# Hybrid attention step: row maxima of mixer A from 64 rows instead of 128, two heads side by side in the two row halves of the array

## The chip, the core and the metric

One core of a Trainium2 chip. The metric is the device time of one execution in microseconds. The engines are named as in the profile: PE multiplies matrices, DVE is the vector engine, ACT the scalar engine, POOL the GpSimd engine, SP issues most DMAs; PEld is PE's weight load, which runs beside its matmuls.

## What is computed

One layer of a diffusion backbone on 128 context tokens (tile 0) and 1024 latent tokens (tiles 1 to 8). After a modulated RMS norm and one input projection there are two attention branches with 8 query heads on 2 key groups each, head size 64. Mixer A is global: each latent query sees all 1024 latent keys and 128 cached context keys. Mixer B sees a window of 128 to either side and the context, with a sink logit. The gated results go through one output projection.

```python
def one_block(qblk):                      # mixer A, per 128 latent queries
    s = jnp.einsum('bqkgd,bskd->bkgqs', qblk, k_all).astype(jnp.float32) * (d ** -0.5)
    p = jax.nn.softmax(s, axis=-1).astype(v_all.dtype)
    return jnp.einsum('bkgqs,bskd->bqkgd', p, v_all)
```

Subtracting any per-row constant before the exponential leaves a softmax unchanged. The kernel subtracts a row maximum of the scores, and that row maximum is what the change touches.

## The kernel before

**Number format.** Every fp32 operand is split into a high part and a low part (`hi`, `lo`), and the products that matter are summed. Queries lie in DRAM as `q_dram[t][m]`, 128 rows: rows 0 to 63 the high parts of the 64 head dimensions, rows 64 to 127 the low parts; the columns are heads, 128 queries each. `u_load` (line 832) brings the four heads of one unit into a tile `qt` of 128 x 512. The keys `kha` hold the high part twice, in rows 0 to 63 and again in 64 to 127, so that a 128-row product gives (q_hi + q_lo) · k_hi.

**Units and slots.** Attention runs over 36 units `(t, m, g)`: token tile, mixer, key group. For each latent tile come unit (A, g0), (B, g0), (A, g1), (B, g1); so an A unit and a B unit alternate, and unit `i` of mixer A has an even number. The four prompt units come last. A unit is a row of slots, one per key block: 9 for mixer A, mostly 4 for mixer B. Below, A0 to A8 are the slots of an A unit and B0 to B3 those of the B unit behind it. The recording loop does in each slot, in this order: what was put off to this slot (`later`), the slot's score matmuls (`scores`), the due items (`due`), some matmuls of the output projection (`po`, 2.5 per slot while there are any), and the value matmuls of the slot three earlier (`values`, LAG = 3). In an A slot the scores are two matmuls (lines 1097 and 1098); `ACT` then takes the exponential (1100) and the high part (1104), and POOL or DVE the low part. In a B slot they are four transposes (1092) of probabilities that were computed earlier. The order in which instructions are recorded is kept on every engine (`in_order`).

**What precedes an A unit.** Its row maxima must be known before its slot A0. For latent tiles, `max_items` makes 12 items out of them, one for each head `h` and each third `b` of the 9 key blocks: a matmul of 128 rows into 384 columns (line 858) and a DVE maximum (859). The table `MX_AT` says in which slots they stand, counted from the start of the A unit two units earlier: five of them in the B unit before that (-4, -3, -2, -2, -1), seven in A4, A5, A5, A7, A7, A8, A8. Then `finish` loads the tile `qb` and takes the negative maximum `m_nat`; two ticks later `transpose` turns it on PE (877, `ptm`) and DVE writes it into four rows of `qb` (878). Units 0 and 2 have their items beside the last gate projection (`EARLY`).

**What precedes a B unit.** `weight_items` puts one head in each of A0 to A3: two matmuls into `sn` (915, 916), a DVE operation with mask and maximum (919), and, from the next slot on, an ACT exponential with its row sum (905, written `pen`, followed by a read of the accumulator). In B1 `pti` (967) turns the inverse sums on PE, and ACT copies them out (971).

**Banks.** The PSUM tag "A" has two banks, taken in turn. In this part of the kernel `pmx`, `sn`, `pti` and `ptm` all take their bank from it: a matmul that writes a bank waits until the last reader of what stood there is done.

Of the kernel before, what the change touches and what calls it, by code (L numbers as in the profile page):

```python
# [9 lines left out]
F32 = mybir.dt.float32  # L10
# [3 lines left out]
ALU = mybir.AluOpType  # L14
AX = mybir.AxisListType
# [3 lines left out]
P = 128  # L19
# [22 lines left out]

NAT_AT = (0, 1, 2, 3)
NAT_FIRST = (0, 1, 2, 3)
MX_AT = (-4, -3, -2, -2, -1, 4, 5, 5, 7, 7, 8, 8)
MX_FIRST = (0, 1, 2, 2, 3, 4, 4, 5, 6, 6, 7, 8)
PH_DVE = 0
MX_END = 10
SPLIT_LAG = 2
# [58 lines left out]
def hybrid_step(ctx, tc, x_prompt, x_sample, cache_k_a, cache_v_a, cache_k_b, cache_v_b,  # L108
# [3 lines left out]
    nc = tc.nc  # L112
# [5 lines left out]
    q_dram = [[dram.tile([P, 1024], F32, name=f"qd{t}_{m}") for m in range(2)] for t in range(NT)]  # L118
# [7 lines left out]
    def later(n, f):  # L126

        agenda.setdefault(now[0] + n, []).append(f)
# [13 lines left out]
    def bank(tag, name):  # L142
        return ps.tile([P, 512], F32, tag=tag, name=name, bufs=BANKS[tag])
# [167 lines left out]
    with tc.tile_pool(name="st", bufs=2, side="right") as st:  # L311
# [129 lines left out]
        for j in range(KT + 2):  # L441
# [42 lines left out]
            if X_FROM + 1 < j <= X_FROM + 4:  # L484
                t = rest[j - X_FROM - 2]
# [8 lines left out]
            if KT - 2 <= j < KT:  # L494
# [3 lines left out]
                c0, n = W_QA.cols[0]  # L498
# [52 lines left out]
    with tc.tile_pool(name="qt", bufs=2, side="right") as qt:  # L551
# [90 lines left out]
        for m in range(2):  # L642
            w, nxt = ((W_QA, W_QB), (W_QB, W_KV))[m]
            ts = list(range(1, NT)) + [0]
            for t in ts:
# [3 lines left out]
                if (m, t) in ((0, ts[-2]), (1, ts[GATE_AT[0]])):  # L649
                    n = len(wg) // 2  # L650
# [28 lines left out]
    kha = kv.tile([P, 2, 9, P], F32R, name="kha")  # L679
# [3 lines left out]
    khp = kv.tile([P, 4, P], F32R, name="khp")  # L683
# [139 lines left out]
    qs = ctx.enter_context(tc.tile_pool(name="qs", bufs=2, side="right"))  # L823
# [5 lines left out]
    qtile, qbtile, mxtile, sgl = {}, {}, {}, {}  # L829
# [4 lines left out]
    def u_load(i):  # L834
        t, m, g = units[i]
        more = i % QTS > 3
        qt_ = (qp2[0] if more else qp).tile([P, 512], F32R, tag="qt", name=f"qt{i}", bufs=QTS - 4 if more else 4)
        nc.sync.dma_start(qt_.bitcast(F32), q_dram[t][m][:, 512 * g : 512 * g + 512])
        qtile[i] = qt_

    def max_items(i):

        t, m, g = units[i]
        out = []

        def item(h, b):
            if h == 0 and b == 0:
                mxtile[i] = qs.tile([P, 4, 3], F32, tag="mx", name=f"mx{i}", bufs=3)
            mx = mxtile[i]
            lhs = qtile[i][:, P * h : P * h + P]  # L850
            pm = bank("A", f"pmx{i}_{h}_{b}")
            if t == 0:
                for h in range(4):
                    hs = slice(P * h, P * h + P)
                    nc.tensor.matmul(pm[:, hs], qtile[i][:, hs], khp[:, g, :], start=True, stop=True)
                nc.vector.tensor_reduce(mx[:, :, 0], pm.rearrange("p (h n) -> p h n", h=4), axis=AX.X, op=ALU.max)
            else:
                nc.tensor.matmul(pm[:, 0:384], lhs, kha[:, g, 3 * b : 3 * b + 3, :], start=True, stop=True)  # L858
                nc.vector.tensor_reduce(mx[:, h, b : b + 1], pm[:, 0:384], axis=AX.X, op=ALU.max)  # L859

        def finish():
            qb_ = qp.tile([68, 512], F32R, tag="qb", name=f"qb{i}", bufs=2)
            nc.sync.dma_start(qb_[0:64, :].bitcast(F32), q_dram[t][m][0:64, 512 * g : 512 * g + 512])
            qbtile[i] = qb_
            mx = mxtile.pop(i)
            mn = m_nat[i // 2 % 2]
            if t > 0:
                m4 = qs.tile([P, 4], F32, tag="m4", name=f"m4{i}", bufs=3)
                nc.vector.tensor_reduce(m4, mx, axis=AX.X, op=ALU.max)
            else:  # L870
                m4 = mx[:, :, 0]
            nc.vector.tensor_scalar(mn, m4, -1.0, None, op0=ALU.mult)
            later(TURN, transpose)

        def transpose():
            pt = bank("A", f"ptm{i}")
            nc.tensor.transpose(pt[0:4, 0:P].bitcast(F32R), m_nat[i // 2 % 2], ident_r)
            nc.vector.tensor_tensor(qbtile[i][64:68, :].rearrange("p (h n) -> p h n", h=4),  # L878
                                    pt[0:4, 0:P].unsqueeze(1).to_broadcast([4, 4, P]),
                                    diag.unsqueeze(2).to_broadcast([4, 4, P]), op=ALU.mult)  # L880

        for h in range(4 if t else 1):
            for b in range(3 if t > 0 else 1):
                out.append(lambda h=h, b=b: item(h, b))
        return out, finish

    def weight_items(i):

# [133 lines left out]
    for i in range(LOADED):  # L1022
        u_load(i)
    for i in EARLY:
        items, end = max_items(i)
        beside[2] += items + [end]
# [14 lines left out]
    for f in beside[2]:  # L1041
# [5 lines left out]
        name=nc.get_next_instruction_name(), engine=mybir.EngineType.Activation, act_func_set_id=6))  # L1047
# [155 lines left out]
    slots, start = [], []  # L1203
# [8 lines left out]
    def put(s, f):  # L1212
        due.setdefault(s, []).append(f)

    for i, (t, m, g) in enumerate(units):
        if i in EARLY:
            continue
        if m == 0:
            items, done = max_items(i)
            at, end = [start[i - 2] + a for a in (MX_AT if i > 2 else MX_FIRST)], start[i - 2] + MX_END  # L1220
            if t == 0:
                end = start[i] - LEAD
                at = [end - 1]
        else:
            items, done = weight_items(i)
            at = [start[i - 1] + j for j in (NAT_AT if i > 1 else NAT_FIRST)] if t else [start[i] - PROMPT_LEAD]
            end = at[-1] + 1
        if i >= LOADED:
            first = max(start[i - QTS + 1] - 1, at[0] - LOADLEAD, 0)
            assert first < at[0] or first == 0, (i, first, at)  # L1230
            put(first, lambda i=i: u_load(i))
        for s, f in zip(at, items):
            put(s, f)
        put(end, done)
# [88 lines left out]
```

## Time and profile before

| | |
|---|---|
| median of 3 runs | 723.58 us (723.54 to 723.71) |
| span of the profiled execution | 721.3 us |
| busy | PE 698.3 us (97%), DVE 457.6 (63%), ACT 411.7 (57%), POOL 335.3 (46%) |
| weight loads (PEld) | 559.7 us (78%) |
| DMA | 78.56 MB, mean 109 GB/s |

The profiled execution has no time of its own beside its span of 721.3 us; the median of the three runs is 2.3 us more than that span, which is what lies around it. Busy times are unions of the instructions' durations on one engine. A matmul's modelled end lies beyond the start of the next one, so the pace of PE is read from the starts: the time from one start to the next.

### The profile page before, as it was taken

Reading aid. Unit: us, or ns where it says so; the run is one execution under the profiler, and the core shown is the slowest. Engines: PE = TensorE matmul, PEld = TensorE weight load, DVE = VectorE, ACT = ScalarE, POOL = GpSimd, SP = SyncE. Lnnn points to the kernel's source line nnn. Section 1 sums busy time; section 2 is a strip of 40 time slices with the busy share of each in tenths; the row PEclk is TensorE's granted clock in tenths of the full one; section 3 lists DMA queues with packets and bytes.
Section 4 is the critical chain, followed back from the end, with each engine's and each line's share of the span. In section 5 each row is a group of like instructions: output and inputs, shape, how many; then the busy total and the mean of one; then the engine's idle time right before and its main releaser. Section 6 shows DMA issues by size and latency. Waiting matters only on the chain. (4 is left out here: it accounts for less than half of the span.)

```text
span 721.3 us, 10622 instructions
## 1 busy us (share of the span) xinstructions
PE 698.3 (97%) x3524; PEld 559.7 (78%) x3524; DVE 457.6 (63%) x1007; ACT 411.7 (57%) x829; POOL 335.3 (46%) x355
## 2 busy tenths in 40 slices
PE   5999999999999999999999999999999999999997
PEld 2678988877777788977788888888888888887865
DVE  3466147875675872745866677577666775775653
ACT  5355411411232451158778877877787778877770
POOL 3456013332322340236666555655575557555751
PEclk9999999999999999999999999999999999999999
DMA  8961373348435115440321222121212221212323
GB/s 344 346 219 59 121 278 86 79 94 276 121 85 142 45 60 171 139 143 23 103 67 45 73 67 88 44 81 52 87 54 59 66 87 45 81 53 87 103 65 119
DMA packets 53159, 78.56 MB, mean 109 GB/s; under 512 B 6569, under 2 KB 25449, under 8 KB 52081
## 3 DMA queue, kind: packets, MB, share of 16 engines
q1 hardware_dynamic: 44928, 65.96, 28.1%
q10 hardware_dynamic: 8176, 11.94, 6.3%
q8 instruction: 28, 0.46, 0.3%
q14 instruction: 27, 0.21, 0.1%
HBM read 58.69 MB, written 19.18 MB: 108 GB/s over the span
## 5 line engine op out<-in xcount | busy, mean ns | idle before, releaser
L1108 POOL TENSOR_TENSOR pl<-pe,ph 128x512 fp32r<-128x512 f32 x130 | 167.6, 1292 | 144.7 <-DVE nm L919 67.5
L859 DVE TENSOR_REDUCE mx<-pmx 128x1 f32<-128x384 f32 x192 | 101.4, 552 | 59.5 <-PE pmx L858 58.1
L1100 ACT ACTIVATE pe<-st 128x512 f32<-128x512 f32 x146 | 86.8, 594 | 28.0 <-PE st L1098 27.1
L1104 ACT CAST ph<-pe 128x512 fp32r<-128x512 f32 x146 | 90.6, 621 | 4.8
L1118 PE MATMUL pv<-ph,v_hi 128*128 128x512 f32 x208 | 83.2, 400 | 2.2 <-DVE spare L1142 2.2
L1121 PE MATMUL pv<-pl,v_hi 128*128 128x512 f32 x208 | 82.6, 397 | 0.0
L173 POOL TENSOR_TENSOR rs_q<-ms_q,mhalf 128x8 f32<-128x8 f32 x18 | 34.8, 1931 | 82.1 <-DVE ms_q L171 82.1
L1189 PE MATMUL po<-wo,ogh 128*128 128x512 f32 x216 | 72.5, 394 | 0.2 <-DVE yt L1196 0.2
L919 DVE CUSTOM_DVE_ANT_0 sn<-sn,mask,nsink 128x512 f32<-128x512 f32 (+1 forms) x64 | 46.3, 724 | 38.3 <-PE sn L916 36.5
L858 PE MATMUL pmx<-kha,qt 128*128 128x384 f32 x192 | 61.0, 363 | 0.4 <-ACT pen L905 0.2
L1097 PE MATMUL st<-qt,kha 128*128 128x512 f32 x144 | 58.3, 405 | 1.5 <-ACT pe L1100 0.8
L1098 PE MATMUL st<-qb,kla 68*128 68x512 f32 x144 | 57.6, 400 | 1.1 <-DVE qb L878 1.1
L1120 PE MATMUL pv<-ph,v_lo 128*64 128x512 f32 x146 | 57.9, 396 | 0.0
L1121 PEld LDWEIGHTS pv<-pl,v_hi 128*128 128x128 f32 x208 | 39.4, 189 | 16.7 <-issue 0.2
L905 ACT ACTIVATE pen<-sn,nm 128x512 f32<-128x512 f32 (+2 forms) x72 | 45.0, 626 | 6.5 <-DVE nm L919 3.1
L1093 ACT CAST ph<-st 128x512 fp32r<-128x512 f32 x62 | 36.4, 587 | 19.9 <-PE st L1092 18.7
L1118 PEld LDWEIGHTS pv<-ph,v_hi 128*128 128x128 f32 x208 | 39.4, 189 | 10.5 <-ACT ogh L1154 2.4
L1189 PEld LDWEIGHTS po<-wo,ogh 128*128 128x128 f32 x216 | 40.0, 188 | 6.8 <-DVE yt L1196 0.6
L1094 DVE TENSOR_TENSOR pl<-st,ph 128x512 fp32r<-128x512 f32 x62 | 42.5, 686 | 2.3 <-ACT ph L1093 1.5
L1189 PE MATMUL po<-wo,ogl 128*128 128x512 f32 x108 | 42.6, 394 | 0.0
L594 ACT ACTIVATE sqq<-pq 128x512 f32<-128x512 f32 x18 | 10.8, 599 | 53.3 <-DMA qd<-qo0q 14.4
L858 PEld LDWEIGHTS pmx<-kha,qt 128*128 128x128 f32 x192 | 35.5, 190 | 6.2 <-DVE mx L859 1.4
(216 smaller groups left out, 1700.2 us busy)
## 6 DMA issues: line engine op xcount, KB each, us to landing
qt<-qd SPq DMA_DIRECT2D x36, 256.0 KB, 3.1
wm<-in_w_mod_ss_dram SPq DMA_DIRECT2D x8, 1024.0 KB, 5.1
qd<-qo0q ACTq DMA_DIRECT2D x36, 128.0 KB, 2.4
qd<-qo1q ACTq DMA_DIRECT2D x36, 128.0 KB, 2.4
sgl<-gd SPq DMA_DIRECT2D x36, 128.0 KB, 2.1
out_dram<-yt SPq DMA_DIRECT2D x17, 256.0 KB, 2.1
xn<-in_x_sample_dram SPq DMA_DIRECT2D x8, 512.0 KB, 7.0
wg<-in_w_mod_g_dram SPq DMA_DIRECT2D x4, 1024.0 KB, 7.9
```

What stands on the lines that cost most here:

```text
L858: nc.tensor.matmul(pm[:, 0:384], lhs, kha[:, g, 3 * b : 3 * b + 3, :], start=True, stop=True)
L859: nc.vector.tensor_reduce(mx[:, h, b : b + 1], pm[:, 0:384], axis=AX.X, op=ALU.max)
L919: nc.vector.tensor_tensor_reduce(s, s, mask[:, m0 : m0 + n], -1.0, nsink[:, 4 * g + h : 4 * g + h + 1], op0=ALU.add, op1=ALU.min, accum_ou ...
L1097: nc.tensor.matmul(s, kh, qtile[i], start=True, stop=False)
L1098: nc.tensor.matmul(s, kl, qbtile[i], start=False, stop=True)
L1100: nc.scalar.activation(pe, s, AF.Exp)
L1104: nc.scalar.copy(ph, pe)
L1108: nc.gpsimd.tensor_tensor(pl, pe, ph, op=ALU.subtract)
L1118: nc.tensor.matmul(pv, two, ph, start=(b == 0), stop=False)
L1120: nc.tensor.matmul(pv[0:64, :], vl, ph, start=False, stop=False)
L1121: nc.tensor.matmul(pv, two, pl, start=False, stop=last)
L1189: nc.tensor.matmul(po[n], a, wo_parts[KT * n + k][lo], start=(k == KS[0] and p == 0), stop=(k == KS[-1] and p == 2))
```

## The change

The maxima of an A unit of a latent tile are now taken from the high parts alone: 64 rows instead of 128. That halves the rows that a head needs, so two heads `2p` and `2p + 1` go at once, one in rows 0 to 63 of the array and one in rows 64 to 127 (`by_rows`). For that, the odd heads' queries must have their high parts in rows 64 to 127: `u_load` loads them with the halves exchanged, in three DMAs per unit in place of one. The other products use all 128 rows, where both halves of the keys are alike. Six items with two matmuls and two DVE maxima each take the place of 12 with one each; each of the two matmuls takes a bank. `MX_AT` has six entries, and the first unit uses the same table. The prompt's maxima stay as they were.

```diff
-MX_AT = (-4, -3, -2, -2, -1, 4, 5, 5, 7, 7, 8, 8)
-MX_FIRST = (0, 1, 2, 2, 3, 4, 4, 5, 6, 6, 7, 8)
+MX_AT = (-4, -3, -1, 4, 6, 8)
@@ u_load
-        nc.sync.dma_start(qt_.bitcast(F32), q_dram[t][m][:, 512 * g : 512 * g + 512])
+        to = qt_.bitcast(F32).rearrange("r (p s n) -> r p s n", s=2, n=P)
+        src = q_dram[t][m][:, 512 * g : 512 * g + 512].rearrange("r (p s n) -> r p s n", s=2, n=P)
+        nc.sync.dma_start(to[:, :, 0], src[:, :, 0])
+        for a in (0, 64):
+            nc.sync.dma_start(to[a : a + 64, :, 1], src[64 - a : 128 - a, :, 1])
@@
+    def by_rows(i, p, keys):
+        return [(qtile[i][64 * s : 64 * s + 64, P * (2 * p + s) : P * (2 * p + s) + P], keys[64 * s : 64 * s + 64])
+                for s in range(2)]
@@ max_items
-        def item(h, b):
...
-                nc.tensor.matmul(pm[:, 0:384], lhs, kha[:, g, 3 * b : 3 * b + 3, :], start=True, stop=True)
-                nc.vector.tensor_reduce(mx[:, h, b : b + 1], pm[:, 0:384], axis=AX.X, op=ALU.max)
+        def item(p, b):
...
+            pms = [bank("A", f"pmx{i}_{2 * p + s}_{b}")[:, 0:384] for s in range(2)]
+            for pm, (q, k) in zip(pms, by_rows(i, p, kha[:, g, 3 * b : 3 * b + 3, :])):
+                nc.tensor.matmul(pm, q, k, start=True, stop=True)
+            for s in range(2):
+                nc.vector.tensor_reduce(mxtile[i][:, 2 * p + s, b : b + 1], pms[s], axis=AX.X, op=ALU.max)
```

Three places show what moves. In the rows, `pmx22_2_0` is the row maximum of unit 22, head 2, third 0; `st20_4` the scores of unit 20, slot 4; `sn`, `pti` and `ptm` are as above, `pv` the values, `po` the output projection; what a row waits for is named by the engine that it waits for.

PE at slot A4 of unit 20, before:

```order
L1097 MATMUL st20_4_6300<-qt20_5728,kha_2319 128x512 [waits Activation_49]
L1098 MATMUL st20_4_6300<-qb20_6148,kla_2320 128x512
L858 MATMUL pmx22_1_2_6309<-kha_2319,qt22_6021 128x384 [waits Activation_49]
L1189 MATMUL po5_1_6286<-wo0_9_3302,ogh16_6003 128x512
L1189 MATMUL po5_1_6286<-wo1_9_3303,ogh16_6003 128x512
L1118 MATMUL pv20_6290<-ph20_1_6231,v_hi_2325 128x512
```

and after:

```order
L1103 MATMUL st20_4_6349<-qt20_5772,kha_2319 128x512 [waits Activation_49]
L1104 MATMUL st20_4_6349<-qb20_6197,kla_2320 128x512
L866 MATMUL pmx22_2_0_6358<-kha_2319,qt22_6069 128x384 [waits Activation_49]
L866 MATMUL pmx22_3_0_6359<-kha_2319,qt22_6069 128x384 [waits Activation_49]
L1195 MATMUL po5_1_6335<-wo0_9_3310,ogh16_6048 128x512
L1195 MATMUL po5_1_6335<-wo1_9_3311,ogh16_6048 128x512
```

One matmul of the maxima stood here, in the bank that head 2 of the B unit's `sn` had used; now two stand here, the second in the bank of head 3, and they are those of heads 2 and 3.

PE from the transposes of slot B0 (unit 19) to the maxima of B1, before:

```order
L1092 MATMUL st19_0_6120<-ident_r_99,pen19_5923 128x128 [waits Activation_49]
L1092 MATMUL st19_0_6120<-ident_r_99,pen19_5923 128x128 x3
L858 MATMUL pmx22_0_0_6129<-kha_2319,qt22_6021 128x384 [waits DMAHW5_49,DVE_49]
L1118 MATMUL pv18_5999<-ph18_6_6057,v_hi_2325 128x512
L1120 MATMUL pv18_5999<-ph18_6_6057,v_lo_2326 64x512
L1121 MATMUL pv18_5999<-pl18_6_6058,v_hi_2325 128x512 [waits Pool_49]
L967 MATMUL pti19_6135<-ident_r_99,inv19_5927 4x128 [waits DVE_49]
L1092 MATMUL st19_1_6140<-ident_r_99,pen19_5923 128x128 [waits Activation_49]
L1092 MATMUL st19_1_6140<-ident_r_99,pen19_5923 128x128 x3
L858 MATMUL pmx22_0_1_6153<-kha_2319,qt22_6021 128x384 [waits DVE_49]
```

and after:

```order
L1098 MATMUL st19_0_6166<-ident_r_99,pen19_5968 128x128 [waits Activation_49]
L1098 MATMUL st19_0_6166<-ident_r_99,pen19_5968 128x128 x3
L866 MATMUL pmx22_0_0_6175<-kha_2319,qt22_6069 128x384 [waits DMAHW7_49,DVE_49]
L866 MATMUL pmx22_1_0_6176<-kha_2319,qt22_6069 128x384 [waits DMAHW1_49,DVE_49]
L1124 MATMUL pv18_6044<-ph18_6_6101,v_hi_2325 128x512
L1126 MATMUL pv18_6044<-ph18_6_6101,v_lo_2326 64x512
L1127 MATMUL pv18_6044<-pl18_6_6102,v_hi_2325 128x512 [waits Pool_49]
L973 MATMUL pti19_6184<-ident_r_99,inv19_5972 4x128 [waits DVE_49]
L1098 MATMUL st19_1_6189<-ident_r_99,pen19_5968 128x128 [waits Activation_49]
L1098 MATMUL st19_1_6189<-ident_r_99,pen19_5968 128x128 x3
L866 MATMUL pmx22_0_1_6202<-kha_2319,qt22_6069 128x384 [waits DVE_49]
L866 MATMUL pmx22_1_1_6203<-kha_2319,qt22_6069 128x384 [waits Activation_49]
```

One matmul of the maxima per slot became two. Around `pti` they now use both banks before it and both behind it, so the second one behind it takes over the bank that ACT reads `pti` from.

PE in slot B3 of unit 19, from the turned maxima of unit 20 on, before:

```order
L877 MATMUL ptm20_6180<-ident_r_99,m_nat0_108 4x128 [waits DVE_49]
L1092 MATMUL st19_3_6187<-ident_r_99,pen19_5923 128x128 [waits PE_49]
L1092 MATMUL st19_3_6187<-ident_r_99,pen19_5923 128x128 x3
L858 MATMUL pmx22_1_1_6195<-kha_2319,qt22_6021 128x384 [waits DVE_49]
L1189 MATMUL po5_0_6174<-wo0_0_3055,ogl16_6004 128x512
```

and after:

```order
L886 MATMUL ptm20_6226<-ident_r_99,m_nat0_108 4x128 [waits DVE_49]
L1098 MATMUL st19_3_6233<-ident_r_99,pen19_5968 128x128 [waits DVE_49,PE_49]
L1098 MATMUL st19_3_6233<-ident_r_99,pen19_5968 128x128 x3
L866 MATMUL pmx22_0_2_6241<-kha_2319,qt22_6069 128x384
L866 MATMUL pmx22_1_2_6242<-kha_2319,qt22_6069 128x384 [waits DVE_49]
L1195 MATMUL po5_0_6220<-wo0_0_3063,ogl16_6049 128x512
```

The one matmul of the maxima here used the bank that `ptm20` does not lie in; now the second of two takes the bank of `ptm20`.

More of the change, by code (lines that the diff above doesn't have):

```diff
@@ L839, in u_load, with prompt @@
         qtile[i] = qt_
+    def by_rows(i, p, keys):
+        return [(qtile[i][64 * s : 64 * s + 64, P * (2 * p + s) : P * (2 * p + s) + P], keys[64 * s : 64 * s + 64])
+                for s in range(2)]
     def max_items(i):
         t, m, g = units[i]
-        out = []
-        def item(h, b):
-            if h == 0 and b == 0:
-                mxtile[i] = qs.tile([P, 4, 3], F32, tag="mx", name=f"mx{i}", bufs=3)
[L849 to L859, printed above, removed]
+        def prompt():
+            mxtile[i] = mx = qs.tile([P, 4, 3], F32, tag="mx", name=f"mx{i}", bufs=3)
+            pm = bank("A", f"pmx{i}")
+            for h in range(4):
+                hs = slice(P * h, P * h + P)
+                nc.tensor.matmul(pm[:, hs], qtile[i][:, hs], khp[:, g, :], start=True, stop=True)
+            nc.vector.tensor_reduce(mx[:, :, 0], pm.rearrange("p (h n) -> p h n", h=4), axis=AX.X, op=ALU.max)
+        def item(p, b):
+            if p == 0 and b == 0:
+                mxtile[i] = qs.tile([P, 4, 3], F32, tag="mx", name=f"mx{i}", bufs=3)
+            pms = [bank("A", f"pmx{i}_{2 * p + s}_{b}")[:, 0:384] for s in range(2)]
[3 more added lines that the diff above has]
+                nc.vector.tensor_reduce(mxtile[i][:, 2 * p + s, b : b + 1], pms[s], axis=AX.X, op=ALU.max)
@@ L880, in transpose @@
                                     diag.unsqueeze(2).to_broadcast([4, 4, P]), op=ALU.mult)
[L882 to L885, printed above, removed]
+        return ([lambda p=p, b=b: item(p, b) for p in range(2) for b in range(3)] if t else [prompt]), finish
     def weight_items(i):
@@ L1219, in hybrid_step @@
             items, done = max_items(i)
-            at, end = [start[i - 2] + a for a in (MX_AT if i > 2 else MX_FIRST)], start[i - 2] + MX_END
+            at, end = [start[i - 2] + a for a in MX_AT], start[i - 2] + MX_END
             if t == 0:
```

## The prediction

> **What bounds the kernel now.** The page comes first, then the busy time by stretches: one from the end of the gate projection to the last units, one with the two early units.
>
> ```profile
> PE 698.3 (97%) x3524; PEld 559.7 (78%) x3524; DVE 457.6 (63%) x1007; ACT 411.7 (57%) x829; POOL 335.3 (46%) x355
> L859 DVE TENSOR_REDUCE mx<-pmx 128x1 f32<-128x384 f32 x192 | 101.4, 552 | 59.5 <-PE pmx L858 58.1
> L858 PE MATMUL pmx<-kha,qt 128*128 128x384 f32 x192 | 61.0, 363 | 0.4 <-ACT pen L905 0.2
> ```
>
> ```profile
> core 0: us, PE busy (x) PEld busy (x) DVE busy (x) ACT busy (x) POOL busy (x), PEclk, DMA share, GB/s
> 378.94:641.33 262.39, 262.39 (x1266) 211.16 (x1266) 182.57 (x388) 205.97 (x408) 154.94 (x165) 1.00 0.22 67
> 282.50:314.80 32.30, 32.30 (x218) 32.11 (x218) 23.14 (x47) 3.60 (x8) 6.45 (x5) 1.00 0.50 155
> ```
>
> The reader is to see that PE never stops from 378.94 to 641.33, at full clock. This stretch is eleven periods of one A unit and one B unit, 262.39 / 11 = 23.85 us each. So whatever PE is spared there shortens the kernel, and whatever it is made to wait lengthens it. The maxima waited 0.4 us in the whole kernel: that they cost PE no more than their own time is due to the place where each stands. I therefore went through one period in the timeline and asked, for each of the new matmuls, when its bank comes free.
>
> **What it removes and what a pair costs.**
>
> ```profile
> 538.37 0.51 PE L858 MATMUL pmx<-kha,qt 128*128 128x384 f32 x2
> 538.71 0.39 PE L1118 MATMUL pv<-ph,v_hi 128*128 128x512 f32 x1
> 538.94 0.40 PE L1120 MATMUL pv<-ph,v_lo 128*64 128x512 f32 x1
> 539.03 1.01 DVE L859 TENSOR_REDUCE mx<-pmx 128x1 f32<-128x384 f32 x2
> 539.18 0.39 PE L1121 MATMUL pv<-pl,v_hi 128*128 128x512 f32 x1
> 539.41 0.60 PE L1092 MATMUL st<-ident_r,pen 128*128 128x128 f32 x4
> 539.76 0.42 PE L858 MATMUL pmx<-kha,qt 128*128 128x384 f32 x1
> 540.02 0.40 PE L1118 MATMUL pv<-ph,v_hi 128*128 128x512 f32 x1
> 540.22 0.56 DVE L859 TENSOR_REDUCE mx<-pmx 128x1 f32<-128x384 f32 x1
> ```
>
> Two matmuls of the maxima take 538.71 - 538.37 = 0.34 to 0.35 us, so 0.175 each; a 512-column matmul takes 0.23, and four transposes 0.44 (540.02 - 539.41 is 0.61, less 0.175). A period has 12 of them: 2.10 us go.
>
> No row of before has two matmuls in two row halves. The nearest ones use column groups:
>
> ```profile
> 58.86 0.39 PE L263 MATMUL pg_f<-h,wloga 128*128 128x512 f32 x1
> 59.18 1.07 PE L350 MATMUL pm<-wm,sil 128*32 128x256 f32 x16
> 60.18 0.74 PE L258 MATMUL pg_f<-h,whiga 128*128 128x512 f32 x2
> 63.49 0.28 PE L258 MATMUL pg_s<-h,whiga 128*128 128x256 f32 x1
> 63.61 0.28 PE L262 MATMUL pg_s<-h,whiga 128*128 128x256 f32 x1
> ```
>
> Sixteen 256-column matmuls in four column groups take 1.00 us, 0.06 each, where one across the whole array takes 0.12: groups do run at once. I take a pair as 0.18 us, one matmul and a start; the other bound is 0.35, if the halves run one after the other. Six pairs are 1.08 us, so 1.02 is spared in a period before any wait. By the Trainium skill (TensorE: Matmul & The Clock Gate, "Measured speedup vs the span model") concurrent tiles cost one matmul and about 4 ns for each further tile, which would put a pair at the 0.18 that I take; it has no run of two row halves at fp32.
>
> Off the path: 72 more DMAs on SP, each unit's load of `qt` now three issues.
>
> ```profile
> qt<-qd SPq DMA_DIRECT2D x36, 256.0 KB, 3.1
> ```
>
> ```profile
> 540.05 0.45 SPq L838 DMA_DIRECT2D qt<-qd x1
> 541.69 0.47 SPq L863 DMA_DIRECT2D qb<-qd x1
> ```
>
> Three issues of 0.45 end by 541.4 and the load by 544.5; this `qt` is first used in the next A0, behind slot B3 (544.09 to 545.5 below). SP is free again before `qb` is issued at 541.69; should it not be, `qb` would be late in B3, which I bound at 0.16 per period and take as nothing. DVE keeps its count of maxima.
>
> **What it adds: waits for banks.** A pair needs both banks of tag A. The price of a wait first:
>
> ```profile
> 353.79 0.68 DVE L878 TENSOR_TENSOR qb<-ptm,diag 4x512 fp32r<-4x512 f32 x1
> 354.52 0.51 PE L1098 MATMUL st<-qb,kla 68*128 68x512 f32 x1 [0.63 <-DVE qb L878]
> 354.87 0.40 PE L915 MATMUL sn<-khb,qt 128*128 128x512 f32 x1
> ```
>
> PE resumes 0.05 us after the release (354.47), and the matmul then takes 0.35 instead of 0.23: its weights could not be loaded ahead, 0.11 more. A second half that had to wait thus ends 0.05 + 0.11 + 0.175 = 0.34 us after its bank's release.
>
> *A4.* The second half takes the bank of `sn` head 3. ACT frees it when its exponential's row sum has been read:
>
> ```profile
> 387.58 0.34 PE L858 MATMUL pmx<-kha,qt 128*128 128x384 f32 x1
> 388.51 0.19 ACT L905 ACTIVATION_READ_ACCUMULATOR pen<-sn,nm 128x1 f32 x1
> ...
> 530.24 0.62 ACT L1104 CAST ph<-pe 128x512 fp32r<-128x512 f32 x1
> 530.72 0.34 PE L858 MATMUL pmx<-kha,qt 128*128 128x384 f32 x1
> 530.77 0.40 ACT L1154 CAST ogh<-spare 128x256 fp32r<-128x256 f32 x1
> 531.08 0.68 ACT L905 ACTIVATE pen<-sn,nm 128x512 f32<-128x512 f32 x1
> 531.66 0.19 ACT L905 ACTIVATION_READ_ACCUMULATOR pen<-sn,nm 128x1 f32 x1
> ...
> 626.13 0.34 PE L858 MATMUL pmx<-kha,qt 128*128 128x384 f32 x1
> 627.07 0.19 ACT L905 ACTIVATION_READ_ACCUMULATOR pen<-sn,nm 128x1 f32 x1
> ```
>
> The read ends at 531.85, 1.13 us after PE is ready for the maxima; it is the same 1.12 to 1.13 in the first (388.70 - 387.58) and the last (627.26 - 626.13) of the eleven periods. ACT is simply behind here: two exponentials and two copies per slot in A0 to A3 stand in its queue ahead of this one. Before, A4 had one matmul, in head 2's bank; the second came in A5. Now PE stands still: the pair ends 1.13 + 0.34 = 1.47 after its start instead of 0.18, loss 1.29. Queued behind it are the projection and the values of A4 and the scores of A5, all of PE's work; the later slots do not give it back, since PE had no gap to give.
>
> *B0.* The pair of A8 starts at p (538.37 in the rows). Its maxima start 0.38 later if DVE is free (0.34 for the matmul and 0.04 to DVE's start, as in 540.18 to 540.22) and end at p + 1.39 (two take 1.01). The pair of B0 could start at p + 0.18 + 0.69 (values) + 0.44 (transposes) = p + 1.31 and would end at 1.49; the second half ends at 1.39 + 0.34 = 1.73. Loss 0.24.
>
> *B1.* The second half takes the bank of `pti`, which ACT copies out:
>
> ```profile
> 540.73 0.27 PE L967 MATMUL pti<-ident_r,inv 128*4 128x128 f32 x1
> 541.04 0.25 ACT L971 COPY spare<-pti 4x128 f32<-4x128 f32 x1 [0.41 <-PE pti L967]
> ```
>
> The copy ends 0.56 after `pti` starts, so the pair ends at 0.90; without the wait it would end at 0.11 + 0.44 + 0.18 = 0.73. Loss 0.17.
>
> *B3.* The second half takes the bank of `ptm`, free when DVE has written `qb`:
>
> ```profile
> 544.09 0.22 PE L877 MATMUL ptm<-ident_r,m_nat 128*4 128x128 f32 x1
> 544.15 0.60 PE L1092 MATMUL st<-ident_r,pen 128*128 128x128 f32 x4
> 544.35 0.68 DVE L878 TENSOR_TENSOR qb<-ptm,diag 4x512 fp32r<-4x512 f32 x1 [0.36 <-PE ptm L877]
> ```
>
> DVE ends 0.94 after `ptm` starts, the pair at 1.28; without the wait at 0.06 + 0.44 + 0.18 = 0.68. Loss 0.60, and up to 0.76 if the load of `qb` lands late. A6 and A8 find both banks free two slots after the last pair: nothing.
>
> **Sum.** Per period -2.10 + 1.08 + 1.29 + 0.24 + 0.17 + 0.60 = +1.28 us. Eleven periods: +14.1. The same for the first two pairs of units, where PE is not full (2.6; bounds 0 and 5), and 1.0 for the last, whose maxima stand before the prompt's units. The early units 0 and 2 have their twelve pairs some 3 us apart beside a PE that is full (32.30 of 32.30) and banks that nothing else uses: -12 x 0.17 = -2.0. Total +15.7 on the profiled 721.3, so 737.0; the median lies 2.3 above the span: 739.3.
>
> **Rivals.** *The waits do not bite: faster.* If ACT, DVE and the copies were in time, only 14 x -1.02 - 2.0 = -16.3 would be left: 707.3. For it: the whole of PE's saving counts, and the change takes no work off it that was hidden. Against it: the point from which it decides is the sum of the waits falling under 1.02 us per period, and A4 alone has 1.29, eleven times alike. ACT would have to read its sum 0.3 us earlier or more, though its queue in A0 to A4 is unchanged. Chance 0.10; a result within 0.2% (1.4 us, about what a measurement here can tell from no change) 0.02.
>
> *The halves run one after the other.* Pairs that do not wait (A6, A8, the twelve early ones) cost 0.35: 14 x 0.34 + 2.0 = 6.8 more, 746. Against it is the row of the sixteen. Chance 0.08.
>
> *Switching the array's division empties it.* Between L263 (58.86) and L350 (59.18) lie 0.32 instead of 0.23, and the second L258 starts 0.34 after the first: 0.09 and 0.11 at a switch. With 0.40 for each undisturbed pair (A6, A8, early) and 0.20 at the end of each waiting one: 14 x 1.6 + 4.8 = 27 more, 766. Against it: 128*64 between 128*128 runs at 0.23 on both sides (538.71 to 539.41), 128*4 likewise, and L350 differs in number format too. Chance 0.08. The Trainium skill (TensorEngine Tiling (Array Packing), "Key Properties") has the rule that a change of tiling mode drains PE. The column rows of this trace disagree with it; for row halves no row decides.
>
> **Chances and range.** The forecast has 0.72; within it the terms give 732 to 745 (waits in B0 to B3 halved or half as large again, the first units from 0 to 5). Slower in all 0.88. The range 731 to 762 takes in the serial halves and half the price of a switch; left out are faster, same and the full price, 0.20.
>
> **What would show it.** Right: a wait of the maxima for ACT's `pen` of about 1.2 us fourteen times, for DVE's `qb` of about 0.5; PE idle some 2 us in a period of 25.1; the two halves starting within 0.02 us in A6. Wrong: `pen` read before the pair in A4, or a gap on both sides of an undisturbed pair.

## The result: 763.4 us, slower by 5.5%

The changed kernel takes 763.45 us (median of 4 runs, 762.38 to 764.15), the kernel before 723.56 (723.30 to 723.71) beside it. The ratio is 1.0547, with a 95% interval from 1.0525 to 1.057. The forecast was 739.3 in a range of 731 to 762: the sign was right, the size was not, and the range missed the result. Experiments ran on other chips or at other times, each beside the kernel before, whose medians there were 723.22 and 723.12. One of the ten runs of the kernel with three loads had a granted clock of 0.85 and took 776 us; it is left out below, and that kernel's profile comes from its second measurement.

The page of the changed kernel, busy times and groups (busy us, mean ns, then idle time ahead of them and what ended it):

```profile
PE 727.2 (96%) x3524; PEld 546.3 (72%) x3524; DVE 453.3 (60%) x1007; ACT 412.6 (54%) x829; POOL 333.9 (44%) x355
L868 DVE TENSOR_REDUCE mx<-pmx 128x1 f32<-128x384 f32 x192 | 99.2, 552 | 95.6 <-PE pmx L866 94.6
L866 PE MATMUL pmx<-kha,qt 64*128 64x384 f32 x192 | 54.1, 437 | 10.3 <-ACT pen L911 8.4
L866 PEld LDWEIGHTS pmx<-kha,qt 64*128 64x128 f32 x192 | 22.9, 183 | 42.2 <-issue 17.9
```

The matmuls of the maxima are still 192, but one lasts 437 ns where it had 363, although it has half the rows. Of 10.3 us of idle time in front of them, 8.4 are the forecast wait for `pen`. The weight loads have 42.2 us of idle time in front of them, and the largest entry, "issue", is idle time in which the engine waited for nothing that the profile shows.

The same eleven periods, by the windows view (columns as in the prediction's: length, then the busy time of PE, PEld, DVE, ACT and POOL with their instructions, the clock, the DMA share and GB/s), and PE's first scores of the first unit, of the first of the periods and behind the last, by the timeline:

```profile
387.15:679.66 292.51, 285.29 (x1266) 203.21 (x1265) 180.04 (x388) 206.96 (x407) 153.70 (x165) 1.00 0.21 60
```

```profile
318.17 0.44 PE L1103 MATMUL st<-qt,kha 128*128 128x512 f32 x1
...
387.15 0.39 PE L1103 MATMUL st<-qt,kha 128*128 128x512 f32 x1
...
679.66 0.40 PE L1103 MATMUL st<-qt,kha 128*128 128x512 f32 x1
```

A period is 292.51 / 11 = 26.59 us, 2.74 more than 23.85, at the same clock of 1.00 and with the same number of instructions. Eleven times that is 30.1 of the 39.9 us in the span (761.2 against 721.3); 8.2 came before (387.15 against 378.94) and 1.6 behind. PE's idle time in the periods, 292.51 - 285.29 = 7.2 us, is the wait for `pen`, 0.66 in each; the rest of the 2.74 has to be read from the starts.

Most of it is seen at A6, where nothing was to be waited for. First PE, then its weight loads:

```profile
559.99 0.40 PE L1103 MATMUL st<-qt,kha 128*128 128x512 f32 x1
560.22 0.40 PE L1104 MATMUL st<-qb,kla 68*128 68x512 f32 x1
560.55 0.44 PE L866 MATMUL pmx<-kha,qt 64*128 64x384 f32 x2
560.92 0.50 PE L1195 MATMUL po<-wo_big,ogl 128*128 128x512 f32 x1
561.25 0.39 PE L1195 MATMUL po<-wo_big,ogh 128*128 128x512 f32 x1
```

```profile
559.99 0.19 PEld L1104 LDWEIGHTS st<-qb,kla 68*128 68x128 f32 x1
560.55 0.19 PEld L866 LDWEIGHTS pmx<-kha,qt 64*128 64x128 f32 x2 [0.37 <-issue]
560.91 0.19 PEld L1195 LDWEIGHTS po<-wo_big,ogl 128*128 128x128 f32 x1 [0.18 <-issue]
561.02 0.19 PEld L1195 LDWEIGHTS po<-wo_big,ogh 128*128 128x128 f32 x1
```

The two halves do run at once: both are in one row of 0.44 us, as long as one matmul, and in the trace the second starts 3 to 4 ns behind the first. But a step from one start to the next is 0.33 ahead of the pair where it should be 0.23, the pair takes 0.37 instead of 0.18, and the matmul behind it 0.33 instead of 0.23. From 560.22 to 561.25 are 1.03 us; 0.23 + 0.18 + 0.23 would be 0.64. So 0.39 us go at an undisturbed pair, and none of it to a semaphore. The loads show why: elsewhere a load starts with the matmul ahead of it (559.99); those of the pair start only with the pair itself, at 560.55, and that of the matmul behind it at 560.91. It is so on both sides of all 66 pairs in the eleven periods: each of these loads starts within 3 ns of its own matmul. By the starts (the ends of matmuls are modelled), PE first becomes empty, about 0.1, and then loads with nothing to hide the load, 0.1 more, once on the way in and once on the way out.

The same stands at B0, behind the transposes:

```profile
565.55 0.60 PE L1098 MATMUL st<-ident_r,pen 128*128 128x128 f32 x4
566.08 0.44 PE L866 MATMUL pmx<-kha,qt 64*128 64x384 f32 x2
566.45 0.50 PE L1124 MATMUL pv<-ph,v_hi 128*128 128x512 f32 x1
566.78 0.39 PE L1126 MATMUL pv<-ph,v_lo 128*64 128x512 f32 x1
```

Here 566.78 - 565.55 = 1.23, against 0.44 + 0.18 + 0.23 = 0.85: 0.38 more. Both banks were free when the pair came (DVE's last maximum of the pair before ends at 565.86), so the wait forecast for B0 is not there.

Of the forecast waits two are left. A4, on PE and ACT:

```profile
555.06 0.40 PE L1104 MATMUL st<-qb,kla 68*128 68x512 f32 x1
...
555.39 0.44 PE L866 MATMUL pmx<-kha,qt 64*128 64x384 f32 x1
...
556.24 0.19 ACT L911 ACTIVATION_READ_ACCUMULATOR pen<-sn,nm 128x1 f32 x1
...
556.49 0.44 PE L866 MATMUL pmx<-kha,qt 64*128 64x384 f32 x1 [0.66 <-ACT pen L911]
...
556.85 0.73 PE L1195 MATMUL po<-wo,ogh 128*128 128x512 f32 x2
```

The second half starts 556.49 - 555.39 = 1.10 after the first, 0.06 behind the end of the read at 556.43. And B3:

```profile
570.94 0.68 DVE L887 TENSOR_TENSOR qb<-ptm,diag 4x512 fp32r<-4x512 f32 x1 [0.96 <-PE ptm L886]
...
571.27 0.84 PE L866 MATMUL pmx<-kha,qt 64*128 64x384 f32 x2
...
571.67 0.18 PEld L866 LDWEIGHTS pmx<-kha,qt 64*128 64x128 f32 x1 [0.22 <-DVE qb L887]
572.04 0.19 PEld L1195 LDWEIGHTS po<-wo,ogl 128*128 128x128 f32 x1 [0.18 <-issue]
```

The second half follows the first by 571.67 - 571.27 = 0.40, at the end of DVE's write of `qb`.

### The profile page after: what moved, and what is told of

Read it like the earlier page. It is cut to its first block, busy times and chain, and to the rows that moved or that the text cites. A ratio compares the mean times of both kernels' runs of the same rounds, so it can differ in the third digit from the quotient of the medians.

```text
span 761.2 us, 10745 instructions
## 1 busy us (share of the span) xinstructions
PE 727.2 (96%) x3524; PEld 546.3 (72%) x3524; DVE 453.3 (60%) x1007; ACT 412.6 (54%) x829; POOL 333.9 (44%) x355
## 5 line engine op out<-in xcount | busy, mean ns | idle before, releaser
L868 DVE TENSOR_REDUCE mx<-pmx 128x1 f32<-128x384 f32 x192 | 99.2, 552 | 95.6 <-PE pmx L866 94.6
L1124 PE MATMUL pv<-ph,v_hi 128*128 128x512 f32 x208 | 87.4, 420 | 2.2 <-DVE spare L1148 2.2
L1195 PE MATMUL po<-wo,ogh 128*128 128x512 f32 x216 | 75.1, 406 | 0.2 <-DVE yt L1202 0.2
L866 PE MATMUL pmx<-kha,qt 64*128 64x384 f32 x192 | 54.1, 437 | 10.3 <-ACT pen L911 8.4
L866 PEld LDWEIGHTS pmx<-kha,qt 64*128 64x128 f32 x192 | 22.9, 183 | 42.2 <-issue 17.9
L1195 PEld LDWEIGHTS po<-wo,ogh 128*128 128x128 f32 x216 | 38.4, 188 | 9.0 <-issue 2.6
```

Of the source, the lines that this page charges most:

```text
L866: nc.tensor.matmul(pm, q, k, start=True, stop=True)
L868: nc.vector.tensor_reduce(mxtile[i][:, 2 * p + s, b : b + 1], pms[s], axis=AX.X, op=ALU.max)
L1124: nc.tensor.matmul(pv, two, ph, start=(b == 0), stop=False)
L1195: nc.tensor.matmul(po[n], a, wo_parts[KT * n + k][lo], start=(k == KS[0] and p == 0), stop=(k == KS[-1] and p == 2))
```

## The experiments

Theory A, formed on these rows: a change between 128-row and 64-row matmuls empties PE and uncovers a weight load, 0.39 us for each stretch of 64-row matmuls (as many as follow each other with no 128-row matmul between), whatever it waits for; the two waits come on top. Rivals: only the waits of the second bank cost (B); the lower half is slow (C); few rows or a weight load of another shape are slow (D); the three loads cost (E); ACT or DVE sets the pace (F).

### 64 rows without pairs, order, banks or loads

```diff
-nc.tensor.matmul(pm[:, 0:384], lhs, kha[:, g, 3 * b : 3 * b + 3, :], start=True, stop=True)
+nc.tensor.matmul(pm[:, 0:384], lhs[0:64], kha[0:64, g, 3 * b : 3 * b + 3, :], start=True, stop=True)
```

> The kernel before with one line changed: each of the 12 maxima contracts rows 0 to 63 alone (array tile 64 x 128, always the upper half), same places, same banks, same loads. Theory A (a change of the array's division empties it; an undisturbed stretch of 64-row matmuls costs 0.39 us beside its own columns): 8 stretches in a period of 23.85, so 3.1 more, in 14 periods 44, and up to 9 for the 24 maxima beside the gate projection: 765 to 777 us. Theory B (only the second bank's waits cost): no order is changed, 723.6 us. Theory C (only matmuls in the lower half, or in two halves, are slow): 723.6 us.

Measured: 775.46 us (774.52 to 776.52), ratio 1.0727 (1.0711 to 1.0743). One line, with every instruction, wait and load in its old place, costs 52 us. PE in the timeline at a single 64-row matmul and at two in a row, and the eleven periods in the windows view:

```profile
566.24 0.40 PE L1098 MATMUL st<-qb,kla 68*128 68x512 f32 x1
566.57 0.44 PE L858 MATMUL pmx<-kha,qt 64*128 64x384 f32 x1
566.94 0.73 PE L1189 MATMUL po<-wo,ogh 128*128 128x512 f32 x2
...
568.42 0.40 PE L1098 MATMUL st<-qb,kla 68*128 68x512 f32 x1
568.75 0.61 PE L858 MATMUL pmx<-kha,qt 64*128 64x384 f32 x2
569.30 0.50 PE L1189 MATMUL po<-wo,ogl 128*128 128x512 f32 x1
569.63 0.62 PE L1189 MATMUL po<-wo_big,ogh 128*128 128x512 f32 x2
```

```profile
396.06:692.70 296.64, 296.64 (x1267) 207.54 (x1266) 181.49 (x388) 207.26 (x407) 154.50 (x165) 1.00 0.19 59
```

At one matmul the steps are 0.33 and 0.37, as at a pair. Two in a row in the same half take 569.30 - 568.75 = 0.55, that is 0.18 more than one: they run one after the other, and the change is paid once. A period is 296.64 / 11 = 26.97, 3.12 more than before; over 8 stretches that is 0.39 each. Theories B and C fall as the whole of the cause: there is no second bank and no lower half here. PE's busy time does not show the loss, since it counts modelled ends: it is 296.64 of 296.64.

### 68 rows

```diff
-nc.tensor.matmul(pm[:, 0:384], lhs, kha[:, g, 3 * b : 3 * b + 3, :], start=True, stop=True)
+nc.tensor.matmul(pm[:, 0:384], lhs[0:68], kha[0:68, g, 3 * b : 3 * b + 3, :], start=True, stop=True)
```

> The kernel before with the maxima contracting rows 0 to 67, four more than a half, so that the array is not divided (tile 128 x 128). Theory A: no change of division, 723.6 us, within 0.2%. Theory D (the number of rows in use, or a weight load of another shape, is what costs): as with 64 rows, 765 us or more.

Measured: 723.24 us (722.14 to 726.04), ratio 1.0006 (0.9995 to 1.0018). The page's group and the eleven periods:

```profile
L858 PE MATMUL pmx<-kha,qt 68*128 68x384 f32 x192 | 60.9, 362 | 0.4 <-ACT pen L905 0.2
```

```profile
378.20:640.48 262.28, 262.28 (x1267) 211.09 (x1266) 182.64 (x388) 206.16 (x408) 154.90 (x165) 1.00 0.21 67
```

262.28 / 11 = 23.84, as before. Four rows more, and the 52 us are gone: what costs comes with the 64-row form, in which two matmuls can run at once, and not with using few rows or loading fewer weights. Theory D falls.

### Three loads

The kernel before with the changed `u_load`, nothing else, in two runs.

> The kernel before, with only the load of the queries changed: three DMAs per unit, odd heads with halves exchanged. All theories but one: hidden, 723.6 us, within 0.2%. Theory E (part of the loss is SP's queue or late queries): 727 us or more, with waits of st or sn for qt or qb in the profile.

> The kernel before with three loads per unit once more, for its profile: 724 to 726 us; if the three issues matter, waits of PE for qt or qb of 1 to 2 us in all, or a longer early part.

Measured: 725.09 us (median of 9 runs, 723.62 to 726.79), ratio 1.0025 (1.0011 to 1.0038), a little more than the 0.2% that were expected, and 724.49 (722.88 to 726.60), ratio 1.0014 (0.9999 to 1.003), as expected. The eleven periods of the second:

```profile
380.63:642.72 262.09, 262.09 (x1266) 211.27 (x1266) 182.26 (x388) 205.85 (x408) 154.91 (x165) 1.00 0.23 67
```

262.09 / 11 = 23.83: the loads are hidden in the periods, as forecast, and PE's waits for `qt` and `qb` are those of the kernel before. What is left, 1 to 2 us, lies ahead of them (380.63 against 378.94); the 68-row kernel, whose loads are the old ones, has 378.20 there, so that these runs do not tell how much of it is the loads'. Theory E falls as a cause of more than these 2 us.

### Pairs on all rows

```diff
-return [(qtile[i][64 * s : 64 * s + 64, P * (2 * p + s) : P * (2 * p + s) + P], keys[64 * s : 64 * s + 64])
+return [(qtile[i][:, P * (2 * p + s) : P * (2 * p + s) + P], keys)
                 for s in range(2)]
```

> The changed kernel with both matmuls of a pair on all 128 rows, one after the other; order, two banks per pair and three loads stay. Theory A: the gaps at both sides of a pair go, and the waits stay; A4 1.12 and B3 0.43 more per period than the kernel before, nothing in B0 and B1, so 14 x 1.55 = 22 more than before at most: 738 to 746 us. Theory B: the pairs lose what the halves spared (0.17 x 96 = 16 us) and keep all waits: 775 to 780 us.

Measured: 745.98 us (743.62 to 746.89), ratio 1.0314 (1.0292 to 1.0336); 17.5 us faster than the changed kernel with twice the work in its maxima. Waits of PE in the eleven periods (us in total, times, longest), and their length:

```profile
PE pmx L866 <- ACT pen L911: 9.4, 11, 0.9
PE pmx L866 <- DVE qb L887: 1.8, 11, 0.2
```

```profile
381.92:660.97 279.05, 267.92 (x1266) 211.39 (x1265) 179.56 (x388) 207.23 (x407) 154.28 (x165) 1.00 0.21 63
```

The two waits stand in every period, and B0 and B1 have none. A period is 25.37: 1.52 above before, where 1.12 + 0.43 = 1.55 was worked out. So the waits are real and cost about what rows say; the halves, meant to pay for them, add 26.59 - 25.37 = 1.22 instead.

### Pairs moved off the waits, with halves and without

```diff
-MX_AT = (-4, -3, -1, 4, 6, 8)
+MX_AT = (-4, -3, -2, 5, 6, 8)
```

The second run has the edit of the section before as well.

> The changed kernel with two of its six pairs one slot off (from B3 to B2, and from A4 to A5), so that neither the read of sn head 3 nor the write of qb stands before a second bank. Theory A (drains and waits add up): the two waits go, 1.04 + 0.40 in 14 periods, 20 us off 763.4: 741 to 747. Theory F (PE is given its pace by ACT or DVE, the waits come back elsewhere): 755 us or more.

> The same places as pairs_freed, with both matmuls of a pair on all 128 rows: neither halves nor waits. Theory A: 723 to 727 us, as the kernel before, since both causes are gone. Theory F: 735 us or more. The difference pairs_freed minus this is the price of the halves alone; theory A has 0.57 - 0.35 = 0.22 for each of 96 pairs, 21 us.

Measured: with halves 748.50 us (747.98 to 753.22), ratio 1.0364 (1.0318 to 1.0411), a little above what was expected; on all rows 731.61 (729.14 to 733.99), ratio 1.0113 (1.0081 to 1.0146), 5 to 9 us above it. The eleven periods of the first and of the second:

```profile
387.81:666.53 278.72, 278.72 (x1267) 198.53 (x1266) 180.25 (x387) 205.98 (x408) 154.16 (x165) 1.00 0.21 63
```

```profile
383.67:649.58 265.91, 265.89 (x1266) 210.47 (x1266) 178.52 (x387) 205.93 (x408) 154.56 (x165) 1.00 0.22 66
```

The periods are 25.34 and 24.17. With the changed kernel and the run on all rows that gives four corners:

| median us (period) | two halves | all rows, in turn |
|---|---|---|
| places as changed | 763.45 (26.59) | 745.98 (25.37) |
| places off the waits | 748.50 (25.34) | 731.61 (24.17) |

The halves cost 17.5 and 16.9 us, the places 15.0 and 14.4, each about the same whatever the other is. For the halves 21 had been expected, 0.22 for each pair; it is 0.20 in the periods (1.22 / 6 and 1.17 / 6). Theory F falls as the main cause: of 1.52 us of waits in a period, moving the full-row pairs off them saves 1.20.

A part of it is real, though. The last corner is still 8.5 us above the kernel before. 0.32 in each of eleven periods are 3.5 of it, and about half of the 0.32 stands at the step into slot A0, which is 0.38 to 0.40 in every period of both moved kernels and 0.23 in the others:

```profile
600.41 0.69 DVE L1100 TENSOR_TENSOR pl<-st,ph 128x512 fp32r<-128x512 f32 x1
...
600.86 0.39 PE L1127 MATMUL pv<-pl,v_hi 128*128 128x512 f32 x1
...
601.22 0.19 PEld L1103 LDWEIGHTS st<-qt,kha 128*128 128x128 f32 x1 [0.40 <-issue]
601.25 0.47 PE L1103 MATMUL st<-qt,kha 128*128 128x512 f32 x1
```

The profile names no wait, but the load starts 0.12 us behind the end of DVE's `pl` (601.10) in every period of these two kernels. In the kernel before it has the same 0.12 (545.06 + 0.69 = 545.75, and 545.87), at a step of 0.23: there PE comes just in time. By this, a wait for DVE took back some 0.15 of what the places gave. Another 0.09 stands behind the pair moved to B2 (598.29 - 597.76 = 0.53, where a pair in B0 or B1 takes 0.44). 4.7 of the 8.5 are lost ahead of the periods (383.67 against 378.94); which of the places costs them was not separated.

### Each pair twice

```diff
-for pm, (q, k) in zip(pms, by_rows(i, p, kha[:, g, 3 * b : 3 * b + 3, :])):
-    nc.tensor.matmul(pm, q, k, start=True, stop=True)
+for _ in range(2):
+    for pm, (q, k) in zip(pms, by_rows(i, p, kha[:, g, 3 * b : 3 * b + 3, :])):
+        nc.tensor.matmul(pm, q, k, start=True, stop=True)
```

> The changed kernel with each pair issued twice in a row into the same two banks (the second overwrites the first with the same values): 96 pairs more, but no more changes of division. Theory A (the price is at the change, and the halves run at once): 0.18 for each, 17 us more than 763.4: 777 to 784. Serial halves: 0.35 each, 797. If every 64-row matmul paid the gap, whatever stands before it: 0.57 each, 818.

Measured: 783.65 us (782.83 to 784.37), ratio 1.0832 (1.0813 to 1.0851). The periods, and PE at a doubled pair:

```profile
394.71:698.98 304.27, 297.02 (x1399) 210.57 (x1397) 179.07 (x388) 206.96 (x407) 153.72 (x165) 1.00 0.19 58
```

```profile
578.38 0.40 PE L1105 MATMUL st<-qb,kla 68*128 68x512 f32 x1
578.71 0.62 PE L867 MATMUL pmx<-kha,qt 64*128 64x384 f32 x4
579.25 0.50 PE L1125 MATMUL pv<-ph,v_hi 128*128 128x512 f32 x1
579.59 0.40 PE L1127 MATMUL pv<-ph,v_lo 128*64 128x512 f32 x1
```

A period is 304.27 / 11 = 27.66: six pairs more cost 1.07, which is 0.178 each. Inside the divided array a pair has the price of one matmul; 0.33 before the four and 0.34 behind them are paid as for two. Serial halves (0.35) and a price at every matmul (0.57) are both out. The other 8 us of the 20 lie outside the periods, most of them ahead (394.71 against 387.15); the 30 pairs that stand there would be 5.3 at the same price, and where the rest goes was not looked at. The Trainium skill (TensorE: Matmul & The Clock Gate, "Measured speedup vs the span model") gives a pack the time of one matmul and some 4 ns per further tile; the 0.178 agrees, but only for a pair with others of its kind around it.

## Why the prediction was right in sign and wrong in size

**What bounds the kernel: right.** The stretch in which PE never stops decided: 30.1 of the 39.9 us are eleven equal periods.

**What is removed, 2.10 per period: not contradicted.** It is a step of the rows of before; no run takes these matmuls out without putting others in. That the sum below closes to 0.07 us speaks for it.

**A pair at 0.18: the step that failed.** 0.178 is the price of a pair among pairs. A pair between 128-row matmuls costs 0.18 + 0.39 = 0.57, more than the upper bound of 0.35 that the prediction gave it, since both bounds took PE to be running. Six pairs are 1.07 + 2.34 a period, not 1.08. The spared 1.02 becomes a loss of 1.3, before any wait. The prediction's own sign of being wrong, a gap on both sides of an undisturbed pair, is what came.

The evidence misread was that on 128\*64 and 128\*4 between 128\*128. It says nothing of rows, and no row shows that a matmul of 64 or 4 columns, alone as it stands there, divides the array at all. The two steps of before that did show 0.09 and 0.11, on both sides of the sixteen matmuls in column groups, were set aside because those differ in number format too, and the switch got a chance of 0.08, though nothing in the trace spoke for row halves being free. The weight loads of before already told the two cases apart, behind the 128\*64 matmul and behind the sixteen:

```profile
538.95 0.19 PEld L1121 LDWEIGHTS pv<-pl,v_hi 128*128 128x128 f32 x1
```

```profile
60.18 0.30 PEld L258 LDWEIGHTS pg_f<-h,whiga 128*128 128x128 f32 x2 [0.41 <-issue]
```

The first starts with the matmul ahead of it (538.94), the second only with its own (60.18), as at the pairs of the changed kernel. Whether the groups or the format held the second is open. The rival's price, 0.40 for each undisturbed pair, was right. That its total of 766 us came so near is in part luck: it put 1.6 us of switches in a period where 2.34 were paid, and kept 2.30 of waits where 1.50 were.

**The waits: right in kind, too large.** A4 was put at 1.29 and is 1.10: the pair itself comes 0.1 later for the switch, and the uncovered load of 0.11 is one that each pair has anyway. B3 was put at 0.60 and is 0.40. B0 was put at 0.24 and B1 at 0.17, and both are nothing, since PE came late to them: the pair of B0 starts 566.08 - 564.37 = 1.71 behind that of A8, where 1.31 was put. In all 1.50 for 2.30. The period by these rows: -2.10 + 1.07 + 2.34 + 1.10 + 0.40 = +2.81; measured +2.74. Moving the pairs off the waits returned 1.25. On all rows the two waits cost 1.52, more than the 1.02 that the forecast spared, so the sign would have been right without the switches as well.

**The early units, -2.0: wrong in sign.** Their pairs have the same price, 12 x (0.57 - 0.35) = +2.6, and their banks were not free: PE waited 0.56 us for DVE's `mx` at 290.15 and 0.64 at 300.49. The first unit starts at 318.17 instead of 314.82. From there to the fourth A unit, where the periods begin, 4.9 us were lost where 2.6 was put; the end lost 1.6 for 1.0.

**The loads as hidden: right in the periods.** Ahead of them PE waited once for a load of `qb`, 0.8 us. The rival of serial halves is refuted by the 0.178, that of waits that do not bite by A4.

**The rival that came true.** By the Trainium skill (TensorEngine Tiling (Array Packing), "Key Properties") a change of tiling mode drains PE. For row halves the runs agree: 0.39 us for going in and out, 0.39 in the kernel with one half alone. For columns the rows of before leave it open, where the prediction took them as against it: the sixteen in column groups have a gap on both sides, while the 128\*64 matmul at 538.94 in the prediction's rows is followed by the next after 0.24.

## What to carry to other kernels

Before dividing the array by rows, count the stretches, not the matmuls: here each stretch of 64-row matmuls cost 0.39 us, and a pair in it spared 0.17, so that three pairs in a row (0.39 + 3 x 0.178 = 0.92 against 1.05) would be the first to gain; that is worked out, not run, as the two banks hold one pair. A price that the trace does not show for the very form at hand needs a rival with a real chance, and a nearby form that is free (64 columns) is no evidence for another (64 rows). And an instruction that needs two buffers at once waits for the later of two owners: look both up.

## What had not been expected

Sixty-four rows were slower than sixty-eight, by 52 us in a kernel of 723 and with about half the array idle in either. And half of the price of a switch, by the starts, is not the emptied array but the weight load behind it: elsewhere it mostly starts a matmul early (559.99 for 560.22), at the switches of the eleven periods never, in either direction. The busy share shows none of it: PE is 96% busy in a kernel that is 5.5% slower.
